# A transformer layer's feed-forward part in blocks of two by two with seven products instead of eight, on one Trainium2 core

## The chip, the core and the metric

The kernel runs on one core of one Trainium2 chip. The time is device microseconds (us) of one execution. The core has five engines with a queue of instructions each: TensorE (PE; its weight loads stand apart as PEld), VectorE (DVE), ScalarE (ACT), GpSimd (POOL) and SyncE (SP). They work side by side and wait for each other through semaphores. Transfers between the chip's main memory (DRAM) and the core's on-chip memory (SBUF) are issued from an engine's queue and carried by 16 DMA engines. TensorE writes its sums into eight accumulators ("banks", each 128 x 512 fp32), which the other engines read.

## The reference

One layer of an encoder, 512 tokens of 2048 features, everything in fp32. The second half of it, which the change is about, is cut out here:

```
proj = rmsnorm(x) @ w_in                  # 2048 x 8704: q, k, v of two attentions, two gates
A = windowed attention, B = neighbourhood attention on the token grid
x = x + (sigmoid(gA) * (A @ w_branch_a) + sigmoid(gB) * (B @ w_branch_b)) @ w_out
h2 = rmsnorm(x)
u = h2 @ w_up                             # 2048 x 11264
u = u[s-1] * cw[0] + u[s] * cw[1] + u[s+1] * cw[2] + conv_b      # along the tokens
gate, val = split(u, 2)                   # 5632 columns each
x = x + (silu(gate) * val) @ w_down       # 5632 x 2048
```

## The kernel before, in words

Activations are held transposed: a tile has 128 features on the partitions and the 512 tokens along the row. Every operand of a product is split into two float32r tiles, `hi` (rounded) and `lo` (the rest), and a product is three matmuls, hi·hi, hi·lo and lo·hi. So a 128 x 128 tile of weights times 512 tokens is three matmuls of 128 x 512, which one line issues (L74).

Weights stream in units of 512 KB. `stage` (L118) takes the next unit off a list that all the steps together make: it issues its load on SP's queue (L71; three `raw` buffers), then ACT's cast to `hi` (L135) and DVE's subtraction to `lo` (L136, 128 x 1024 each, two buffers each). `run_step` (L146) calls `stage` once per unit, ahead of the 24 matmuls of the unit that it uses itself, so that weights are always prepared one unit early, and at the end of a step it hands each of the four banks to the step's `evac`. A step makes 512 output columns. A list of queued closures (`run_queued`) runs attention's small work between units.

The order of the program: w_in's attention columns with the attentions (to about 600 us), gates of A, branch A, gates of B, branch B, output projection with the residual, and then the feed-forward part from about 1194 us on: `up` (L583) makes a chunk of 512 gate and 512 value columns, `conv` (L573) their evacuation, and `down` (L606) the product of one chunk earlier with the matching rows of w_down, added to the residual `x2` in SBUF (L610). In `conv`, DVE multiplies the bank by the norm's row factor (L575), ACT makes the middle tap with the bias (L576), and DVE adds the two outer taps (L577, L579). The sigmoid (L589) and the products of gate and value (L590, L595) follow, and `split` (L180, L181) makes the tiles for `down`.

The instruction order on each engine comes from a scheduler that simulates the program; loads through `dma` keep the program's order.

## Time and profile before

| what | value |
|---|---|
| median of 3 runs | 2634.89 us (2634.71 to 2635.88) |
| span of the profiled execution | 2634.1 us, 28831 instructions |
| TensorE busy | 2623.6 us (100%), granted clock 1.000 |
| weight loads | 2182.7 us (83%) |
| VectorE busy | 1258.4 us (48%) |
| ScalarE busy | 840.8 us (32%) |
| DMA, mean | 102 GB/s |

The profiled execution's own time is its span, from the first to the last instruction; it lies 0.8 us under the median of the runs. Times that are worked out from the trace go by the span. In a group's row, the columns behind the bar are the busy time of all its instructions, the mean time of one in ns, and how long the engine stood idle just before them and for what. The busy time of TensorE counts overlapping matmuls' ends, so the distance from one matmul to the next is read from a stretch of them, and not from the mean time of one.

### The profile page before, as it was taken

The page shows a single profiled execution, that of the slowest core. Times are in us where ns is not written, and L with a number is a line of the kernel's source. Part 1 is how long each engine was busy: PE and PEld are TensorE (multiplying, and loading weights), DVE is VectorE, ACT ScalarE, POOL GpSimd, SP SyncE. Part 2 cuts the span into 40 slices and gives each one's busy share as a digit, 9 for nine tenths or more (in the row PEclk, how much of TensorE's full clock was granted, in tenths as well). Part 3 has the DMA queues.
Part 4 walks back from the last instruction along what each step waited for, and adds up shares of the span by engine and source line. Part 5 has one row for each costly group of instructions (what it writes and reads, how often), then busy time and mean ns, then how long its engine had stood idle before and what let it go on. Part 6 is the DMA issues. An engine that isn't in the chain of part 4 may idle for free.

```text
span 2634.1 us, 28831 instructions
## 1 busy us (share of the span) xinstructions
PE 2623.6 (100%) x11848; PEld 2182.7 (83%) x11848; DVE 1258.4 (48%) x1685; ACT 840.8 (32%) x1156; POOL 34.4 (1%) x38
## 2 busy tenths in 40 slices
PE   9999999999999999999999999999999999999999
PEld 7888888888888888888888888888888888888887
DVE  6565545542333344435453636363636363636364
ACT  5355544532222222323232323231323232323231
POOL 0100000000000000000000000000000000000000
PEclk9999999999999999999999999999999999999999
DMA  5322222333233323332323232333333333332333
GB/s 181 96 89 85 90 94 90 114 107 115 98 96 96 112 96 127 113 114 94 96 96 101 95 100 97 96 96 96 96 97 98 100 97 96 96 97 96 96 96 128
DMA packets 152115, 268.53 MB, mean 102 GB/s; under 512 B 9520, under 2 KB 35120, under 8 KB 151984
## 3 DMA queue, kind: packets, MB, share of 16 engines
q1 hardware_dynamic: 147376, 258.31, 30.7%
q10 hardware_dynamic: 4608, 8.39, 0.8%
q8 instruction: 92, 1.51, 0.2%
q14 instruction: 39, 0.32, 0.0%
HBM read 258.27 MB, written 8.39 MB: 101 GB/s over the span
## 4 chain that ended last, share of the span: by engine, by line
PE 100%; DMA 0%; DVE 0%; ACT 0%; issue 0%; SPq 0%; ACTq 0%
PE mm L74 96%; PE tr L74 2%; PE tr L430 1%; PE tr L288 0%; PE tr L337 0%; DMA s<-in_x_t 0%; PE mm L217 0%; PE tr L217 0%; PE mm L208 0%; ACT s L183 0%; DVE s L514 0%; DVE s L610 0%; PE tr L208 0%; ACT hi L135 0%; SPq L71 0%
## 5 line engine op out<-in xcount | busy, mean ns | idle before, releaser
L74 PE MATMUL mm<-s,hi 128*128 128x512 f32 x6528 | 1937.0, 389 | 0.9 <-DVE s L514 0.9
L74 PEld LDWEIGHTS mm<-s,hi 128*128 128x128 f32 x6528 | 1224.5, 188 | 253.7 <-ACT s L524 1.3
L74 PE MATMUL mm<-s,lo 128*128 128x512 f32 x3264 | 1193.7, 389 | 0.0
L136 DVE TENSOR_TENSOR lo<-raw,hi 128x1024 fp32r<-128x1024 f32 (+1 forms) x465 | 568.1, 1222 | 1161.7 <-ACT hi L135 1159.1
L135 ACT CAST hi<-raw 128x1024 fp32r<-128x1024 f32 (+1 forms) x465 | 489.1, 1052 | 1507.3 <-PE mm L74 1332.7
L74 PEld LDWEIGHTS mm<-s,lo 128*128 128x128 f32 x3264 | 612.6, 188 | 126.6
L74 PE MATMUL mm<-hi,s 128*128 128x512 f32 x896 | 285.5, 395 | 5.8 <-ACT hi L135 5.8
L74 PEld LDWEIGHTS mm<-hi,s 128*128 128x128 f32 x896 | 168.6, 189 | 39.0 <-ACT hi L135 5.8
L74 PE MATMUL mm<-lo,s 128*128 128x512 f32 x448 | 176.8, 396 | 0.0
L610 DVE TENSOR_TENSOR e<-mm,e 128x512 f32<-128x512 f32 x132 | 90.1, 689 | 23.5 <-PE mm L74 23.2
L74 PEld LDWEIGHTS mm<-lo,s 128*128 128x128 f32 x448 | 84.9, 190 | 16.5
L576 ACT ACTIVATE s<-t,smalls 128x512 f32<-128x512 f32 x88 | 71.4, 811 | 42.6 <-DVE t L575 42.6
L577 DVE SCALAR_TENSOR_TENSOR s<-t,smalls,s 128x511 f32<-128x511 f32 x88 | 65.8, 748 | 10.1 <-ACT s L576 9.7
L579 DVE SCALAR_TENSOR_TENSOR s<-t,smalls,s 128x511 f32<-128x511 f32 x88 | 65.9, 749 | 2.4
L575 DVE TENSOR_TENSOR t<-mm,row 128x512 f32<-128x512 f32 x88 | 60.4, 687 | 2.4 <-PE mm L74 2.4
L435 DVE TENSOR_TENSOR pl<-tr,ph 128x256 fp32r<-128x256 f32 (+1 forms) x64 | 30.2, 485 | 29.7 <-ACT ph L434 29.6
L589 ACT ACTIVATE t<-s 128x512 f32<-128x512 f32 x44 | 27.8, 631 | 51.0 <-DVE s L579 51.0
L409 ACT ACTIVATE p<-p,nm 128x256 f32<-128x256 f32 (+1 forms) x64 | 35.4, 555 | 23.8 <-DVE nm L402 15.9
L434 ACT CAST ph<-tr 128x256 fp32r<-128x256 f32 (+1 forms) x64 | 26.1, 421 | 47.4 <-PE tr L74 22.1
L610 DVE TENSOR_TENSOR s<-mm,s 128x512 f32<-128x512 f32 x44 | 30.4, 692 | 19.9 <-PE mm L74 19.9
L74 PE MATMUL tr<-ph,s 128*128 128x256 f32 (+1 forms) x128 | 37.7, 313 | 0.0
L180 ACT CAST s<-s 128x512 fp32r<-128x512 f32 x52 | 32.0, 619 | 17.5 <-DVE s L531 9.7
(102 smaller groups left out, 849.8 us busy)
## 6 DMA issues: line engine op xcount, KB each, us to landing
raw<-in_w_up SPq DMA_DIRECT2D x176, 512.0 KB, 3.5
raw<-in_w_in SPq DMA_DIRECT2D x103, 512.0 KB, 3.6
raw<-in_w_down SPq DMA_DIRECT2D x88, 512.0 KB, 3.6
raw<-in_w_in SPq DMA_DIRECT2D x66, 256.0 KB, 3.1
raw<-in_w_out SPq DMA_DIRECT2D x32, 512.0 KB, 3.7
raw<-in_w_branch_a SPq DMA_DIRECT2D x16, 512.0 KB, 3.6
raw<-in_w_branch_b SPq DMA_DIRECT2D x16, 512.0 KB, 3.7
s<-in_x_t SPq DMA_DIRECT2D x20, 256.0 KB, 6.1
```

What stands on the lines that cost most here:

```text
L74: nc.tensor.matmul(o, l, r, start=start, stop=stop, skip_group_check=True)
L135: nc.scalar.copy(hi[:, c:c + n], raw[:, c:c + n])
L136: nc.vector.tensor_tensor(lo[:, c:c + n], raw[:, c:c + n], hi[:, c:c + n].bitcast(F32), ALU.subtract)
L180: nc.scalar.copy(hi, src)
L409: nc.scalar.activation(pr[j][:, :n], pr[j][:, :n], AF.Exp, bias=nm[:, j:j + 1], accum_out=sm[:, j:j + 1])
L435: nc.vector.tensor_tensor(pl[:, :n], b[:, :n], ph[:, :n].bitcast(F32), ALU.subtract)
L575: nc.vector.tensor_tensor(u, ps, rows["f"], ALU.mult)
L576: nc.scalar.activation(o, u, AF.Identity, bias=cb[:, idx:idx + 1], scale=cw[:, idx, 1:2])
L577: nc.vector.scalar_tensor_tensor(o[:, 1:], u[:, :S - 1], cw[:, idx, 0:1], o[:, 1:], op0=ALU.mult, op1=ALU.add)
L579: nc.vector.scalar_tensor_tensor(o[:, :S - 1], u[:, 1:], cw[:, idx, 2:3], o[:, :S - 1], op0=ALU.mult, op1=ALU.add)
L589: nc.scalar.activation(sg, g, AF.Sigmoid)
L610: nc.vector.tensor_tensor(x2[m], ps, x2[m], ALU.add)
```

## The change

The feed-forward products are made in blocks of two by two: two tiles of features by two halves of the weight columns on the one side, two tiles of features by two halves of 256 tokens on the other. For w_up the two column halves are the gate and the value columns; for w_down they are the two halves of its 2048. Instead of eight block products there are seven, each of a sum of weight blocks with a sum of activation blocks (Strassen's scheme in Winograd's form), and the four output blocks are sums of the seven.

- **Weights.** `Twin` loads two units at once: four planes of 128 x 512, 256 KB each. `add` makes three further planes on DVE out of them (L568 on 1024 elements, L570 and L571 on 512), which makes seven. `Product.prep` casts one unit's seven planes to `wh` on ACT (L612, 1024 and 768 elements) and subtracts to `wl` on DVE (L613, likewise).
- **Early sums.** For the first two up steps and for all of w_down (52 twins) the sums are made ahead, by `make_early` in the stretch between the attentions and the feed-forward part: load, `add`, and a store of four planes (1 MB) on GpSimd's queue (L581). They are read back when they are needed (1 MB of sums beside three raw planes).
- **Activations.** `forms` makes the seven blocks of a pair of tiles: 4 sums on DVE, 7 casts on ACT (L630) and 7 subtractions on DVE (L631), all 128 x 256. There are 30 pairs (8 for w_up, 22 for w_down).
- **Products.** A step has one bank for each of the seven products, and for each unit 7 x 2 x 3 = 42 matmuls of 128 x 256 (L77). There are 22 up steps of eight units, each giving two tiles of gate and two of value, and then 12 down steps (two parts of four steps with eight units, one of four with six): 11,088 matmuls of 128 x 256 in place of 6,336 of 128 x 512. Outside the feed-forward part the matmuls are the same.
- **Evacuation.** `combine` makes the four output blocks with one copy on ACT (L674) and seven sums on DVE (L675 to L681, 512 elements each). In `conv`, DVE multiplies by the row factor (L825, 1024 elements), and ACT makes all three taps (L829, L831, L832, two instructions each). The outer taps are added to the middle one by two DMAs on GpSimd's queue that accumulate in SBUF (L833, L834). Silu (L849), the product of gate and value (L850) and a store to DRAM (L851, GpSimd's queue) follow; `form_down` reads it back.
- **Down.** All up steps come first. The residual lies in DRAM (`total`); a down step's results are added to it by accumulating DMAs on GpSimd's queue, and in the last part by DVE ahead of the output.
- **Around it.** Branch A comes right after the first half of its gates, and its heads are read back and split just ahead of it (`before_a`); the other half of the gates is applied afterwards. There are 56 instead of 60 activation slots, and the raw stream's buffers give their place to the product weights' (`wst_ctx.close()`, in `post` of the last output step).

The diff, cut to its core:

```diff
+UP_EARLY = (0, 1)
...
+    def prep_to(n, **kw):
+        for u in units[at["prep"]:n + 1]:
+            if isinstance(u, Product) and "w" not in ffn:
+                return
+            u.prep(**kw)
+            at["prep"] += 1
+    def advance():
+        prep_to(at["use"] + 1)
+        while at["sums"] < len(twins) and twins[at["sums"]].first <= at["use"] + 2:
+            if "f" not in ffn:
+                return
+            twins[at["sums"]].sums()
+            at["sums"] += 1
+        while at["load"] < len(twins) and twins[at["load"]].first <= at["use"] + 4:
+            if at["early"] < len(early):
+                break
+            twins[at["load"]].load()
+            at["load"] += 1
+        make_early()
...
+    class Twin:
+        def __init__(self, w, d, c, first, kept):
+            self.w, self.first = w[d][:, :, :, :, c:c + 256], first
+            self.kept = kept and dram.tile([P, 4, 512], F32, name=f"sums{first}")
+        def fetch(self, *planes):
+            self.f = ffn["f"].tile([P, 7, 512], F32, tag="f", name="f", bufs=2)
+            for f, a, h in ((0, 0, 0), (1, 1, 0), (3, 0, 1), (6, 1, 1)):
+                if f in planes:
+                    dma(self.f[:, f].rearrange("p (b n) -> p b n", b=2), self.w[:, :, a, h])
+        def load(self):
+            if self.kept:
+                self.fetch(0, 1, 6)
+                dma(self.f[:, 2:6], self.kept)
+            else:
+                self.fetch(0, 1, 3, 6)
+        def add(self):
+            f = self.f
+            nc.vector.tensor_tensor(
+                f[:, 2:4], f[:, 0:7:6], f[:, 3].unsqueeze(1).to_broadcast([P, 2, 512]), ALU.add)
+            nc.vector.tensor_tensor(f[:, 4], f[:, 2], f[:, 6], ALU.add)
+            nc.vector.tensor_tensor(f[:, 5], f[:, 4], f[:, 1], ALU.add)
...
+        def keep(self):
+            nc.gpsimd.dma_start(self.kept, self.f[:, 2:6])
+    def make_early():
+        if "f" not in ffn or at["early"] == len(early) and not made:
+            return
+        if made and made[0][1] == 1:
+            made.popleft()[0].keep()
+        elif made and made[0][1] == 0 and (len(made) == 2 or at["early"] == len(early)):
+            made[0][0].add()
+            made[0][1] = 1
+            return
+        while len(made) < 2 and at["early"] < len(early):
+            t = early[at["early"]]
+            t.fetch_all()
+            made.append([t, 0])
+            at["early"] += 1
+    class Product:
+        def __init__(self, twin, i):
+            self.twin, self.s = twin, slice(i * 256, i * 256 + 256)
+        def prep(self):
+            self.parts = []
+            for tag, a, b in (("a", 0, 4), ("b", 4, 7)):
+                hi = ffn["w"].tile([P, b - a, 256], F32R, tag="h" + tag, name="wh", bufs=2)
+                lo = ffn["w"].tile([P, b - a, 256], F32R, tag="l" + tag, name="wl", bufs=2)
+                f = self.twin.f[:, a:b, self.s]
+                nc.scalar.copy(hi, f)
+                nc.vector.tensor_tensor(lo, f, hi.bitcast(F32), ALU.subtract)
+                self.parts += [(hi[:, i], lo[:, i]) for i in range(b - a)]
+    def forms(src):
+        y = src.rearrange("p j (t n) -> p (j t) n", t=2)
+        t = quad("o").rearrange("p j (t n) -> p (j t) n", t=2)
+        nc.vector.tensor_tensor(t[:, 0], y[:, 3], y[:, 1], ALU.subtract)
+        nc.vector.tensor_tensor(t[:, 1], y[:, 0], y[:, 1], ALU.subtract)
+        nc.vector.tensor_tensor(t[:, 2], t[:, 0], y[:, 0], ALU.add)
+        nc.vector.tensor_tensor(t[:, 3], t[:, 2], y[:, 2], ALU.subtract)
+        res = []
+        for v in (y[:, 0], y[:, 2], t[:, 0], t[:, 1], t[:, 2], y[:, 3], t[:, 3]):
+            o = slot(F32R)
+            nc.scalar.copy(o[:, :256], v)
+            nc.vector.tensor_tensor(o[:, 256:], v, o[:, :256].bitcast(F32), ALU.subtract)
+            res.append(o)
+        return res
+    def products(w, c, pairs, acts, evac, before=None, kept=False):
+        def run():
+            ps = []
+            for i, j in enumerate(pairs):
+                if before:
+                    before(i)
+                u = next_unit()
+                for f, (wh, wl) in enumerate(u.parts):
+                    if i == 0:
+                        ps.append(bank("mm"))
+                    a = acts[j][f]
+                    for m in range(2):
+                        o, s = ps[f][:, m * 256:(m + 1) * 256], slice(m * P, (m + 1) * P)
+                        mm(o, wh[:, s], a[:, :256], i == m == 0, False)
+                        mm(o, wh[:, s], a[:, 256:], False, False)
+                        mm(o, wl[:, s], a[:, :256], False, i == len(pairs) - 1 and m == 1)
+                if i == len(pairs) - 1:
+                    combine(ps, evac)
+                advance()
+                run_queued(1)
+            if before:
+                before(len(pairs))
+        steps.append(run)
+        v = w.rearrange("(d b a p) (h n) -> d p b a h n", b=2, a=2, p=P, h=2)
+        for j in pairs[::2]:
+            t = Twin(v, j // 2, c, len(units), kept)
+            twins.append(t)
+            units.extend(Product(t, i) for i in range(2))
+            if kept:
+                early.append(t)
+    def combine(ps, evac):
+        q1, q2, q7, q5, q6, q3, q4 = [p.rearrange("p (m n) -> p m n", m=2) for p in ps]
+        v = lambda: scratch().rearrange("p (m n) -> p m n", m=2)
+        top, low, p1, u3 = quad("u"), quad("u"), v(), v()
+        left, right = slice(0, 256), slice(256, 512)
+        nc.scalar.copy(p1, q1)
+        nc.vector.tensor_tensor(top[:, :, left], q2, p1, ALU.add)
+        nc.vector.tensor_tensor(p1, p1, q6, ALU.subtract)
+        nc.vector.scalar_tensor_tensor(u3, q7, -1.0, p1, op0=ALU.mult, op1=ALU.subtract)
+        nc.vector.tensor_tensor(low[:, :, right], u3, q5, ALU.subtract)
+        nc.vector.tensor_tensor(p1, p1, q5, ALU.add)
+        nc.vector.tensor_tensor(top[:, :, right], q3, p1, ALU.add)
+        nc.vector.tensor_tensor(low[:, :, left], u3, q4, ALU.subtract)
+        evac(top, low)
...
+    def before_a():
+        end_attention()
+        split_out(oa, out_a)
...
+        def post():
+            if n == 3:
+                wst_ctx.close()
+                ffn["w"] = ctx.enter_context(
+                    tc.tile_pool(name="w", bufs=2, side="right", reuse_waits="tile"))
+                prep_to(at["use"] + 1)
+                form_pair(6)
+                form_pair(7)
...
+    pairs_ff = D_FF // 256
+    act = [dram.tile([P, 2, S], F32, name=f"act{j}") for j in range(pairs_ff)]
+    def conv(u, idx):
+        o, before, after = quad("o"), quad("a"), quad("a")
+        nc.vector.tensor_tensor(
+            u, u, rows["f"].unsqueeze(1).to_broadcast([P, 2, S]), ALU.mult)
+        for m in range(2):
+            i = idx + m
+            nc.scalar.activation(
+                o[:, m], u[:, m], AF.Identity, bias=cb[:, i:i + 1], scale=cw[:, i, 1:2])
+            nc.scalar.activation(before[:, m], u[:, m], AF.Copy, scale=cw[:, i, 0:1])
+            nc.scalar.activation(after[:, m], u[:, m], AF.Copy, scale=cw[:, i, 2:3])
+        nc.gpsimd.dma_start(o[:, :, 1:], before[:, :, :S - 1], accum_op=ALU.add)
+        nc.gpsimd.dma_start(o[:, :, :S - 1], after[:, :, 1:], accum_op=ALU.add)
         return o
+            def out_part():
+                g, v = held["g"], held["v"]
+                nc.scalar.activation(g, g, AF.Silu)
+                nc.vector.tensor_tensor(v, g, v, ALU.mult)
+                nc.gpsimd.dma_start(act[s], v)
+            queue.extend((gate_part, lambda: None, lambda: None, val_part,
+                          lambda: None, lambda: None, out_part))
+        def before(i):
+            if s == 0 and i == 5:
                 rows["f"] = row_factor("f")[1]
+            if s == pairs_ff - 1 and i >= 1:
+                form_down(0, i - 1)
+        products(w_up, s * 256, range(8), h2, evac, before=before, kept=s in UP_EARLY)
...
+    def down(part, pairs, nxt=()):
+        last = not nxt
+        skip = len(pairs) - len(nxt)
+        for s in range(4):
+            old = []
+            def evac(top, low, s=s, old=old):
+                for h, t in enumerate((top, low)):
+                    if not last:
+                        nc.gpsimd.dma_start(total[h][s], t, accum_op=ALU.add)
+                    else:
+                        nc.vector.tensor_tensor(t, t, old[h], ALU.add)
+                        m = 8 * h + 2 * s
+                        nc.scalar.dma_start(
+                            out[m * P:(m + 2) * P].rearrange("(m p) n -> p m n", p=P), t)
+            def before(i, s=s, old=old):
+                if last and i == len(pairs) - 2:
+                    for h in range(2):
+                        old.append(quad("a"))
+                        dma(old[h], total[h][s])
+                if s == 3:
+                    for n in FORM[part][i]:
+                        form_down(part + 1, n)
+            products(w_down, s * 256, pairs, down_forms[part], evac, before=before, kept=True)
+    down_forms = {0: {}, 1: {}, 2: {}}
+    def form_down(part, j):
+        a = quad("a")
+        dma(a, act[j])
+        down_forms[part][j] = forms(a)
+    FORM = {0: [()] + [(8 + i,) for i in range(8)],
+            1: [()] + [(16 + i,) for i in range(6)] + [(), ()],
+            2: [()] * 9}
+    for s in range(pairs_ff):
+        up(s)
+    down(0, range(0, 8), range(8, 16))
+    down(1, range(8, 16), range(16, 22))
+    down(2, range(16, 22))
```

**VectorE at the end of a step.** Before, where four gate or value banks are evacuated (t: scratch, s: activation slot, row: the row factor):

```order
L575 TENSOR_TENSOR t_9610<-mm_9335,row_9204 128x512
L595 TENSOR_TENSOR s_9576<-s_9296,s_9576 128x512
L136 TENSOR_TENSOR lo_9548<-raw_9546,hi_9547 128x1024
L181 TENSOR_TENSOR s_9584<-s_9576,s_9583 128x512
L577 SCALAR_TENSOR_TENSOR s_9587<-t_9588,smalls_94,s_9587 128x511
```

With the change, where the seven banks of an up step are combined (f: a twin's planes, wh and wl: prepared weights, u: the combined blocks):

```order
L676 TENSOR_TENSOR t_12623<-t_12623,mm_12211 128x512
L613 TENSOR_TENSOR wl_12634<-f_12413,wh_12633 128x1024
L570 TENSOR_TENSOR f_12521<-f_12521 128x512
L613 TENSOR_TENSOR wl_12638<-f_12413,wh_12637 128x768
L677 SCALAR_TENSOR_TENSOR t_12624<-mm_12197,t_12623 128x512
L571 TENSOR_TENSOR f_12521<-f_12521 128x512
L678 TENSOR_TENSOR u_12622<-t_12624,mm_12204 128x2x256
L679 TENSOR_TENSOR t_12623<-t_12623,mm_12204 128x512
L681 TENSOR_TENSOR u_12622<-t_12624,mm_12225 128x2x256
L613 TENSOR_TENSOR wl_12711<-f_12521,wh_12710 128x1024
L680 TENSOR_TENSOR u_12621<-mm_12218,t_12623 128x2x256
```

Weight preparation and weight sums stand between the seven sums that free the banks.

**TensorE at the start of a step.** Before, a new step's matmuls begin in four other banks than the ones just finished (mm_9032 is the last bank of the step before):

```order
L74 MATMUL mm_9032<-s_9022,hi_9207 128x512
L74 MATMUL mm_9032<-s_9023,hi_9207 128x512
L74 MATMUL mm_9032<-s_9022,lo_9208 128x512
L74 MATMUL mm_9332<-s_8147,hi_9237 128x512
L74 MATMUL mm_9332<-s_8148,hi_9237 128x512
```

With the change, twelve rows behind the last matmul of the step before:

```order
L77 MATMUL mm_12675<-s_8760,wh_12571 128x256 x2
L77 MATMUL mm_12675<-s_8760,wl_12572 128x256
L77 MATMUL mm_12661<-s_8888,wh_12633 128x256 x2
L77 MATMUL mm_12668<-s_8891,wh_12633 128x256 x2
L77 MATMUL mm_12675<-s_8894,wh_12633 128x256 x2
L77 MATMUL mm_12682<-s_8763,wh_12571 128x256 x2
```

Seven of eight banks are in use in a step. The first three products of the step's first unit and then parts of its second unit (wh_12633) stand ahead of the first unit's fourth product (mm_12682).

**ScalarE and GpSimd behind a step.** Before, a middle tap stood between two casts (L135) at a time. With the change, ScalarE has, behind the three taps of the first of two gate tiles:

```order
L829 ACTIVATE o_13127<-u_13099,smalls_98 128x512
L831 ACTIVATE a_13128<-u_13099,smalls_98 128x512
L832 ACTIVATE a_13129<-u_13099,smalls_98 128x512
L829 ACTIVATE o_13304<-u_13100,smalls_98 128x512 x2
L612 CAST wh_13358<-f_13122 128x1024
L612 CAST wh_13300<-f_13122 128x768
L612 CAST wh_13362<-f_13122 128x768
L831 ACTIVATE a_13305<-u_13100,smalls_98 128x512 x2
```

and GpSimd's queue, for one up step:

```order
L833 DMA o_10737<-a_10738 128x2x511
L834 DMA o_10737<-a_10739 128x2x511
L833 DMA o_10914<-a_10915 128x2x511
L834 DMA o_10914<-a_10916 128x2x511
L851 DMA act1_134<-o_10914 128x1024
```

Eight tap instructions now stand between two casts (the three ahead of these rows and the first five here), and the store of a step's product (L851) stands behind its four adding transfers.

257 lines of the change are left out of this document (143 added, 114 removed).

## The prediction

> **What bounds the kernel now.** First the page's busy shares with the granted clock, and the chain of work that ended last with its last long step, whose columns are start, length, engine and work:
>
> ```profile
> span 2634.1 us, 28831 instructions
> PE 2623.6 (100%) x11848; PEld 2182.7 (83%) x11848; DVE 1258.4 (48%) x1685; ACT 840.8 (32%) x1156; POOL 34.4 (1%) x38
> PEclk9999999999999999999999999999999999999999
> PE 100%; DMA 0%; DVE 0%; ACT 0%; issue 0%; SPq 0%; ACTq 0%
> ...
> 1227.18 1403.09 PE mm L74 x6190
> ```
>
> TensorE is never kept waiting, and its clock is full throughout. 1403.09 us for 6190 matmuls is 0.2267 us for each of 512 columns. Next, busy times by stretch (columns: stretch, length, then busy time and count of PE, PEld, DVE, ACT, POOL; clock, DMA share, GB/s): the one ahead of the feed-forward part, and that part:
>
> ```profile
> 600.00:1190.00 590.00, 590.00 (x2604) 488.55 (x2603) 218.30 (x242) 155.91 (x182) 0.00 (x0) 1.00 0.33 106
> 1193.80:2630.00 1436.20, 1436.20 (x6346) 1189.34 (x6344) 702.84 (x844) 395.38 (x442) 1.93 (x1) 1.00 0.31 98
> ```
>
> The feed-forward part is 1436.2 us, 55% of the span, with DVE at 49%. So only less TensorE work shortens it, and DVE has as much room again.
>
> **The change, part by part.**
>
> *TensorE.* 6336 matmuls of 512 columns become 11,088 of 256. These exist before only in the attention; rows of several in a stretch, where one row's time is (n - 1) distances and one whole matmul, then the matmul alone (the mean in its group), and the shortest kind of load and matmul:
>
> ```profile
> 131.68 0.75 PE L74 MATMUL tr<-s 128*128 128x256 f32 x5
> 254.92 0.53 PE L74 MATMUL tr<-s 128*128 128x256 f32 x3
> L74 PE MATMUL tr<-s 128*128 128x256 f32 x96 | 17.0, 281 | 0.0
> 1219.27 0.95 PE L208 MATMUL mm<-ones,sq 128*128 128x1 f32 x8
> ```
>
> (0.75 - 0.281) / 4 = 0.117 us, (0.53 - 0.281) / 2 = 0.125, and for eight loads with one column each about (0.95 - 0.239) / 7 = 0.10. Half of 0.2267 is 0.113. I take 0.118, near the longer stretch: 11,088 x 0.118 = 1308 us, 128 under 1436. An up step (8 x 42 matmuls) is then at least 39.65 us.
>
> *DVE and ACT in an up step.* What the pieces cost, by their nearest rows:
>
> ```profile
> L136 DVE TENSOR_TENSOR lo<-raw,hi 128x1024 fp32r<-128x1024 f32 x463 | 566.8, 1224 | 1161.7 <-ACT hi L135 1159.1 <-PE mm L74 2.2
> L595 DVE TENSOR_TENSOR s<-s 128x512 f32<-128x512 f32 x44 | 30.2, 687 | 0.8
> L610 DVE TENSOR_TENSOR e<-mm,e 128x512 f32<-128x512 f32 x132 | 90.1, 689 | 23.5 <-PE mm L74 23.2
> L281 DVE TENSOR_TENSOR qr<-t 128x256 f32<-128x256 f32 x8 | 3.4, 420 | 0.0
> L135 ACT CAST hi<-raw 128x1024 fp32r<-128x1024 f32 x463 | 487.8, 1054 | 1507.3 <-PE mm L74 1332.7 <-issue 170.9 <-DMA raw<-in_w_in 1.1
> L326 ACT COPY s<-mm 128x512 f32<-128x512 f32 x8 | 4.7, 583 | 4.1 <-PE mm L74 4.1
> L576 ACT ACTIVATE s<-t,smalls 128x512 f32<-128x512 f32 x88 | 71.4, 811 | 42.6 <-DVE t L575 42.6
> L577 DVE SCALAR_TENSOR_TENSOR s<-t,smalls,s 128x511 f32<-128x511 f32 x88 | 65.8, 748 | 10.1 <-ACT s L576 9.7
> L183 ACT ACTIVATE s<-e,smalls 128x512 fp32r<-128x512 f32 x12 | 8.6, 715 | 5.8 <-DVE e L563 5.8
> ```
>
> 768 elements on DVE: halfway, (1.224 + 0.687) / 2 = 0.955. Per step, DVE has eight preparations, 8 x (1.224 + 0.955) = 17.4; four twins' sums, 4 x (1.224 + 2 x 0.687) = 10.4; seven sums of `combine`, 7 x 0.69 = 4.8; two row factors and the product of gate and value, 3 x 1.224 = 3.7. Sum 36.3 us, 92% of TensorE's 39.65. ACT: 8 x (1.054 + 0.82) = 15.0 for casts (768 again halfway, with 0.583 at 512), 0.6 for the copy, 4 x 0.811 + 8 x 0.715 = 9.0 for twelve taps, 1.05 for Silu: 25.7, 65%.
>
> The outer taps leave DVE (eight of L577's form, 8 x 0.748 = 6.0, which would have put it over TensorE), the weight sums come on. What margin is left can be used up by waiting. In the program's order a step's first matmuls need three banks that `combine` frees, its fourth product waits for L677, the fifth for L679, the seventh for L680. Walked with the times above, L677 ends 2.9 us into the step against 2.8 when TensorE gets there, L679 5.9 against 5.7, L680 8.5 against 9.2: about even, since preparation stands between these sums on DVE's queue, and a late sum holds TensorE with everything behind it. Two things then idle DVE itself. ACT's four middle and four outer taps, 4 x 0.811 + 4 x 0.715 = 6.1 us, stand ahead of a cast that DVE's next subtraction waits for; it has 3.5 us of other work in that time, so 2.6 are lost. And the planes of a twin have two buffers: a new megabyte can only be asked for when the last subtraction of the twin two earlier is done. Landing times:
>
> ```profile
> raw<-in_w_up SPq DMA_DIRECT2D x176, 512.0 KB, 3.5
> raw<-in_w_in SPq DMA_DIRECT2D x66, 256.0 KB, 3.1
> s<-in_x_t SPq DMA_DIRECT2D x20, 256.0 KB, 6.1
> q1 hardware_dynamic: 147376, 258.31, 30.7%
> out_a<-o ACTq DMA_DIRECT2D x8, 256.0 KB, 2.0
> ```
>
> Four planes of 256 KB take between 3.5 (a 512 KB transfer) and 6.1 us (loads that queue up in fours); I take 4.5, against 2.9 us of work that DVE has meanwhile: 1.6 lost. With 1 us of handing over between ACT and DVE, DVE's loop is 36.3 + 2.6 + 1.6 + 1 = 41.5 us, and a step 42, at worst 44. Bounds: 39.65 if order and buffers absorb all of it. Steps 0 and 1 have their sums ready: 40.5.
>
> *Down.* A pair's forms are 4 sums and 7 subtractions of 256 elements at 0.420. Counted in the order of DVE's instructions from one step's `combine` to the next one's, with these prices, DVE has 40.7 us in the last up step (14 of the forms' subtractions of part 0), 55.8 in the first down step (42 of them), 40.1 to 40.3 in three later ones (25 to 31 each), and 18 to 25 in the other eight, where it sets nothing. I take 43 for that up step, 57, 3 x 42, 4 x 40.6 (TensorE's 39.65 and a wait for a bank) and 4 x 30.5 for steps of six units (252 x 0.118 = 29.7): 57 + 126 + 162 + 122 = 467. Up is 2 x 40.5 + 19 x 42 + 43 = 922. Together 1389 us, 47 under 1436 and 81 over the floor. Bounds: the floor below; 2 us more in each of 30 steps, 1450, above.
>
> *Ahead of it.* Branch A's heads are read back and split right ahead of its matmuls, which nothing covers: +3 us. The weights' pool takes the raw stream's place only after the last output matmul; the first cast and subtraction (2.3 us) and a late twin: +6. The early sums: 52 x (1.224 + 2 x 0.687) = 135 us of DVE in a stretch of 590 where it is busy 218, so hidden; its traffic rises from 106 GB/s by 2 MB for every second unit (10.9 us), 192 GB/s, to about 300, where the queue's 258 MB in 30.7% of the span make 320 GB/s at full use. Raw loads then queue behind a twin's on SP, but are asked for a unit early: 0 taken, up to 30 us if it fails.
>
> *The end.* Before, the last matmul is followed by
>
> ```profile
> 2630.30 0.69 DVE L610 TENSOR_TENSOR s<-mm,s 128x512 f32<-128x512 f32 x1 [0.67 <-PE mm L74]
> 2627.85 3.51 ACTq L612 DMA_DIRECT2D out_x<-s  x4
> ```
>
> With the change by the copy, the chain of `combine`, two additions of 1024 elements (0.6 + 4 x 0.69 + 2 x 1.2 = 5.8) and a 512 KB store, 3.5 to 4: 10 us, before about 4.
>
> Sum: 1194 + 3 + 6 + 1389 + 10 = **2602 us** of span, 32 under 2634.1; the runs' median stands 0.8 above the span, so 2603.
>
> The Trainium skill, "TensorE: Matmul & The Clock Gate", section "Wait — 56ns, not 53.3ns?", says that with hardware decoding off TensorE's sequencer spends about 62 ns on each matmul; if a weight load costs the same, a pair would take 124 ns, an estimate from that page, and 11,088 of them 1375 us, 67 more than my floor. The row at 131.68 us shows 0.117 per pair, which speaks against it, but five pairs may have been queued ahead.
>
> **Rivals.**
>
> 1. *The order absorbs everything:* TensorE never waits. For it: before, DVE held it hardly ever. Against: 92% is not 49%. 1194 + 3 + 1308 + 10 = 2515, with 0.115 per matmul 2482.
>
> 2. *The adding DMAs are late (slower than before).* In `conv` the outer taps are two transfers of 128 x 2 x 511 elements on GpSimd's queue, one behind the other, and the second waits for the first; Silu, the gate product and the release of the `o`, `a` and `u` buffers wait for them, and the next step's `combine` needs `u`. The value pair's are issued some 27.8 us into the step, and the gate product (L850) stands on DVE's queue at 34.4, with the next unit's subtraction behind it: they have 6.5 us for two. No row shows an accumulating transfer or one on this queue. Plainly, 512 packets of 88 ns over 16 engines (147,376 packets in 30.7% of 16 x 2634 us) are 2.8 us, a 512 KB load lands in 3.5, the loads in fours in 6.1. Each us beyond 6.5 is a us of TensorE in 22 steps: at 8 us, +33, the gain is gone; at 10 us, 2603 + 77 = 2680. For it: reading the destination as well doubles the traffic. Against: 6.5 us is over twice the plain price. The Trainium skill warns of this in "SBUF — State Buffer", section "SBUF: two separate sides": GpSimd's DMA descriptors are starved while DVE holds the port that they share. No run shows it here.
>
> 3. *The shorter matmul is dearer:* the row at 254.92 us with its 0.125. For it: it is as much a row as the other, and a five-in-a-row stretch may draw on matmuls that were queued ahead. Against: the two rows' ends are rounded to 0.01 us, which over two distances is 0.005 each. 1194 + 3 + 11,088 x 0.125 + 10 = 2593 without waits, and with half of the forecast's 81 us of waits (a slower TensorE needs the banks later) and the 6 us at the start about 2640, no gain.
>
> 4. *The early sums choke the raw stream,* or something not listed: 2603 + 30, up to 2690.
>
> **How the numbers follow.** Forecast 0.42 (own range 2575 to 2630); order absorbs everything 0.22; adding DMAs or the DVE chain late 0.22; dearer matmul 0.08; early sums and the rest 0.06. The range of 8 in 10 runs from 2535, since a partly absorbed step of 40.5 is 2570 and the floor 2515 holds a part of the second case, to 2690 for the third. This kernel's measurement can tell 0.2%, 5.3 us, from no change. Faster: the forecast nearly whole, the second, and little of the others: 0.62; within 0.2% 0.06; slower 0.32.
>
> **What would show it.** TensorE's share falls under 100%, and the 128 x 256 groups show their idle time as released by DVE, L677 and L679 above all; the distance between steps' first matmuls is about 42 us, with DVE busy near 90% of it. A step of 39.7 shows the first rival. A landing time of the `o<-a` transfers above 6.5 us, with L850 idle for DMA, shows the second; a distance of 0.125 within a unit, without idle time, the third. Gaps of TensorE for `raw` between 600 and 1190 us show the fourth. I am wrong if DVE is under 85% and TensorE waits all the same.

## The result: slower by 6%

The changed kernel takes 2793.06 us (2786.35 to 2800.03, 4 runs) against 2635.38 us before: a ratio of 1.0599, 95% interval 1.0581 to 1.0617. The forecast was 2603 us, with 2690 as its upper end.

The head of its page answers to the first three rows that the prediction began with:

```profile
span 2789.6 us, 41803 instructions
PE 2604.5 (93%) x16600; PEld 2358.9 (85%) x16600; DVE 1748.1 (63%) x2399; ACT 1206.8 (43%) x1783; POOL 202.6 (7%) x232
PEclk9999999999999999999999999999999988999999
```

TensorE's busy time fell by only 19 us, and it now stands idle for 185. The first row below is the stretch ahead of the feed-forward part (compare 600 to 1190 us before); then come the up steps, the first down step, and the other down steps:

```profile
600.00:1200.00 600.00, 569.94 (x2399) 455.56 (x2399) 326.52 (x396) 151.93 (x189) 31.72 (x59) 0.99 0.81 282
1262.64:2284.70 1022.06, 925.56 (x7368) 908.50 (x7369) 725.49 (x848) 519.04 (x673) 111.04 (x103) 0.96 0.58 148
2284.70:2361.30 76.60, 48.14 (x353) 47.52 (x352) 48.61 (x95) 41.12 (x79) 7.69 (x7) 0.80 0.73 213
2361.30:2780.40 419.10, 407.93 (x3387) 404.31 (x3385) 275.14 (x400) 183.13 (x268) 14.27 (x17) 1.00 0.73 228
```

| part, us | before | forecast | changed kernel |
|---|---|---|---|
| up to the first feed-forward matmul | 1193.8 | 1203 | 1262.6 |
| up steps | | 922 | 1022 |
| down steps | | 467 | 496 |
| feed-forward part | 1436 | 1389 | 1518 |
| behind the last matmul | 4 | 10 | 9 |

So both parts lost: 69 us ahead of the feed-forward part, 82 in it. An up step, from one `combine` to the next, is 46.86 us on the mean of 20, where TensorE's own work is 336 x 0.119 = 40.0 (0.119 us is the distance of two matmuls that wait for nothing).

Who keeps whom waiting in the up steps (columns: us in all, times, longest), TensorE, then VectorE, then ScalarE:

```profile
PE mm L77 <- DVE wl L613: 43.0, 29, 5.4
PE mm L77 <- ACT wh L612: 38.9, 21, 7.6
PE mm L77 <- DVE t L676: 13.0, 11, 4.5
...
DVE wl L613 <- ACT wh L612: 125.3, 33, 11.1
DVE f L568 <- DMA f<-in_w_up: 103.1, 45, 6.0
DVE o L850 <- DMA o<-a: 39.5, 15, 5.1
...
ACT a L832 <- DMA o<-a: 74.3, 20, 7.5
...
ACT a L831 <- DMA o<-a: 44.1, 16, 4.7
```

TensorE waits far more for prepared weights (the first two rows, 81.9 us) than for free banks (the third, 13.0). The three rows are 94.9 us, 4.5 in each of 21 steps; of the rest of the 6.9 us above 40.0, the lower clock can explain up to 0.04 x 46.9 = 1.9, since 0.96 was granted over these steps. VectorE waits for ScalarE's casts, and ScalarE, ahead of them on its queue, for the adding DMAs (`o<-a`), whose `a` buffers it fills again. Beside that VectorE waits at the weight sums (L568) for planes that are on their way, and at the gate product (L850) for the adding DMAs. Rows of one step, each engine's in order of time: GpSimd's queue, then those of ScalarE and VectorE that bear on it, then TensorE's one long wait:

```profile
1838.25 1.17 POOL L833 DMA_DIRECT2D o<-a  x1 [19.61 <-ACT a L831]
1845.63 1.18 POOL L834 DMA_DIRECT2D o<-a  x1 [6.20 <-ACT wh L612]
1846.81 1.22 POOL L833 DMA_DIRECT2D o<-a  x1
1856.46 1.18 POOL L834 DMA_DIRECT2D o<-a  x1 [8.42 <-DMA o<-a]
...
1851.10 1.34 ACT L832 ACTIVATE a<-u,smalls 128x512 f32<-128x512 f32 x2 [2.88 <-DMA o<-a]
...
1842.68 1.23 DVE L568 TENSOR_TENSOR f<-f 128x1024 f32<-128x1024 f32 x1 [4.05 <-DMA f<-in_w_up]
...
1854.14 1.83 DVE L613 TENSOR_TENSOR wl<-f,wh 128x768 fp32r<-128x768 f32 x2 [3.89 <-ACT wh L612]
1857.70 1.22 DVE L568 TENSOR_TENSOR f<-f 128x1024 f32<-128x1024 f32 x1 [1.73 <-DMA f<-in_w_up]
1863.90 1.23 DVE L850 TENSOR_TENSOR o<-o 128x1024 f32<-128x1024 f32 x1 [4.97 <-DMA o<-a]
...
1865.65 1.22 DVE L613 TENSOR_TENSOR wl<-f,wh 128x1024 fp32r<-128x1024 f32 x1
...
1866.92 0.58 PE L77 MATMUL mm<-s,wl 128*128 128x256 f32 x1 [5.37 <-DVE wl L613]
```

Four adding transfers fill nearly all the time from 1838.3 to 1863.9 us, 25.6 us of a step of 46.9; the third is issued 1.2 us behind the second, the second and the fourth only when the one ahead has landed. ScalarE's L832 of the value half waits for the gate's second one, casts stand behind it, and L613 at 1854.14 is late by that. L850 waits for the last one, and the L613 behind L850 is what ends TensorE's wait of 5.4 us.

### The profile page after: what moved, and what is told of

Its sections match the earlier page's. It is cut to its first block, busy times and chain, and to the rows that moved or that the text cites. A ratio compares the mean times of both kernels' runs of the same rounds, so it can differ in the third digit from the quotient of the medians.

```text
span 2789.6 us, 41803 instructions
## 1 busy us (share of the span) xinstructions
PE 2604.5 (93%) x16600; PEld 2358.9 (85%) x16600; DVE 1748.1 (63%) x2399; ACT 1206.8 (43%) x1783; POOL 202.6 (7%) x232
## 5 line engine op out<-in xcount | busy, mean ns | idle before, releaser
L77 PE MATMUL mm<-s,wh 128*128 128x256 f32 x7392 | 1316.4, 287 | 87.1 <-ACT wh L612 72.4
L77 PEld LDWEIGHTS mm<-s,wh 128*128 128x128 f32 x7392 | 1123.6, 193 | 97.8 <-ACT wh L612 78.6
L77 PE MATMUL mm<-s,wl 128*128 128x256 f32 x3696 | 963.6, 287 | 51.5 <-DVE wl L613 50.9
L612 ACT CAST wh<-f 128x1024 fp32r<-128x1024 f32 (+1 forms) x528 | 480.7, 938 | 566.8 <-PE mm L77 391.2
L613 DVE TENSOR_TENSOR wl<-f,wh 128x1024 fp32r<-128x1024 f32 (+1 forms) x528 | 564.6, 1089 | 256.9 <-ACT wh L612 249.9
L77 PEld LDWEIGHTS mm<-s,wl 128*128 128x128 f32 x3696 | 669.7, 192 | 62.5 <-DVE wl L613 61.2
L77 PE MATMUL mm<-s,hi 128*128 128x512 f32 x2304 | 700.7, 397 | 5.2 <-ACT hi L151 3.0
L77 PEld LDWEIGHTS mm<-s,hi 128*128 128x128 f32 x2304 | 436.1, 190 | 105.7 <-ACT hi L151 4.0
L77 PE MATMUL mm<-s,lo 128*128 128x512 f32 x1152 | 430.5, 400 | 26.9 <-DVE lo L152 26.9
L152 DVE TENSOR_TENSOR lo<-raw,hi 128x1024 fp32r<-128x1024 f32 (+1 forms) x201 | 244.2, 1218 | 239.9 <-ACT hi L151 239.1
L568 DVE TENSOR_TENSOR f<-f 128x1024 f32<-128x1024 f32 x132 | 161.6, 1224 | 273.7 <-DMA f<-in_w_down 166.0
L77 PE MATMUL mm<-hi,s 128*128 128x512 f32 x896 | 289.5, 399 | 5.6 <-ACT hi L151 5.6
L77 PEld LDWEIGHTS mm<-s,lo 128*128 128x128 f32 x1152 | 219.4, 190 | 83.9 <-DVE lo L152 34.2
L77 PEld LDWEIGHTS mm<-hi,s 128*128 128x128 f32 x896 | 168.6, 190 | 41.8 <-ACT hi L151 5.6
L77 PE MATMUL mm<-lo,s 128*128 128x512 f32 x448 | 178.7, 400 | 0.0
L77 PEld LDWEIGHTS mm<-lo,s 128*128 128x128 f32 x448 | 85.1, 190 | 18.4
L832 ACT ACTIVATE a<-u,smalls 128x512 f32<-128x512 f32 x88 | 60.5, 712 | 74.3 <-DMA o<-a 74.3
L570 DVE TENSOR_TENSOR f<-f 128x512 f32<-128x512 f32 x132 | 90.9, 689 | 1.5
L571 DVE TENSOR_TENSOR f<-f 128x512 f32<-128x512 f32 x132 | 90.9, 689 | 1.4
L833 POOL DMA_DIRECT2D o<-a x44 | 53.4, 1214 | 511.6 <-ACT a L831 410.0
L831 ACT ACTIVATE a<-u,smalls 128x512 f32<-128x512 f32 x88 | 60.5, 713 | 44.6 <-DMA o<-a 44.1
```

Of the source, the lines that this page charges most:

```text
L77: nc.tensor.matmul(o, l, r, start=start, stop=stop, skip_group_check=True)
L152: nc.vector.tensor_tensor(lo[:, c:c + n], self.raw[:, c:c + n], hi[:, c:c + n].bitcast(F32), ALU.subtract)
L568: nc.vector.tensor_tensor(f[:, 2:4], f[:, 0:7:6], f[:, 3].unsqueeze(1).to_broadcast([P, 2, 512]), ALU.add)
L570: nc.vector.tensor_tensor(f[:, 4], f[:, 2], f[:, 6], ALU.add)
L571: nc.vector.tensor_tensor(f[:, 5], f[:, 4], f[:, 1], ALU.add)
L612: nc.scalar.copy(hi, f)
```

## The experiments

A run without a ratio beside it is a single one. The four runs of the changed kernel lie up to 14 us apart, so a span that differs by less than that shows nothing by itself; the starts and steps within a trace are what the readings go by.

**The up steps: adding DMAs or the planes' reload.** First each of the two is left out. Without the adding DMAs:

```
-        nc.gpsimd.dma_start(o[:, :, 1:], before[:, :, :S - 1], accum_op=ALU.add)
-        nc.gpsimd.dma_start(o[:, :, :S - 1], after[:, :, 1:], accum_op=ALU.add)
```

> Left out: the two adding DMAs of each conv (L833, L834), so that the outer taps are computed on ScalarE but never added. With them an up step takes 46.8 us (2284.7 - 1301.4 over 21 steps). Theory A (four adding transfers, one behind the other from 1838.3 to 1863.9 us in the step looked at, hold ScalarE's L831/L832 and VectorE's L850, and through them the casts): a step falls to 41 to 42.5 us, the span by 90 to 125 us. Theory B (the reload of the weight planes, for which L568 waits 5.8 us in that step, sets the pace): the step stays above 45 us, the span falls by less than 40.

Measured: 43.42 us a step, a span of 2701.1 us (-88.5; the first down step is shorter too, 62 us against 77). Neither theory's figure: half of the excess is gone. Without the loads:

```
-                self.fetch(0, 1, 3, 6)
+                if len(held_f) < 2:
+                    self.fetch(0, 1, 3, 6)
+                    held_f.append(self.f)
+                else:
+                    held_f.append(held_f.pop(0))
+                    self.f = held_f[-1]
```

> Left out: the loads of w_up for the up steps from the third on; two tiles of planes are loaded once and used again and again (the sums are still made each time). Theory A: the step stays at 45 us or more, since the adding transfers stay. Theory B: 41 to 42.5 us. If both waits lie side by side and each alone is enough, both this run and the one without adding DMAs stay near 45.

Measured: 42.96 us a step, span 2705.8. Again a little over half of it. Both edits together:

> The changed kernel without the adding DMAs and without the loads of w_up from the third up step on. If the two waits in the up steps lie one behind the other, their gains add: from 46.8 us a step minus 3.0 (without the adding DMAs alone) and minus 4.4 (without the loads alone) is 39.4, which is under TensorE's 336 x 0.119 = 40.0, so 40 to 40.5. If they hide each other or share a third cause (the order of VectorE's work, its 36.3 us), the step stays at 42 or more.

Measured: 40.32 us a step, span 2637.3. Between 1320 and 2040 us TensorE has no gap left:

```profile
1320.00:2040.00 720.00, 720.00 (x6003) 720.00 (x6002) 603.16 (x679) 425.79 (x533) 9.64 (x18) 1.00 0.06 20
```

So the two waits, with the clock that they cost, are nearly the whole excess of the up steps: 3.4 and 3.9 us alone, 6.5 together. The transfers also slow each other, as the landing times show (columns: count, KB each, median us from issue to landing; the changed kernel, then without the loads, then without the adding DMAs, all from 1320 to 2200 us):

```profile
f<-in_w_up SPq DMA_DIRECT2D x300, 256.0 KB, 4.4
o<-a POOLq DMA_DIRECT2D x75, 511.0 KB, 6.7
```
```profile
o<-a POOLq DMA_DIRECT2D x82, 511.0 KB, 4.8
act<-o POOLq DMA_DIRECT2D x20, 512.0 KB, 2.9
```
```profile
f<-in_w_up SPq DMA_DIRECT2D x323, 256.0 KB, 4.0
```

An adding transfer lands in 4.8 us without the loads beside it and in 6.7 with them; a plain store of nearly the same size on the same queue takes 2.9 in both runs. The Trainium skill, "DMA: Bandwidth & Descriptors", section "Anatomy of one DMA — SWDGE (gpsimd) path", fits 2.0 us and the bytes at 436 GB/s for that queue, 3.2 us for 512 KB as an estimate from it: near the plain store, while the adding transfer takes half as much again. It also differs from the store in staying within SBUF, so how much of that is the adding isn't shown.

Was the reload a matter of the order on VectorE's queue? The sums are held behind the last subtraction issued so far:

```
-            if not self.kept:
-                self.add()
+            if not self.kept:
+                with tc.issue_after(last["prep"]) if "prep" in last else ExitStack():
+                    self.add()
```

> The changed kernel; one thing is added: a twin's three sums must stand on VectorE's queue behind the last weight subtraction (L613) issued so far, so that L568 no longer stands ahead of subtractions that could run while its planes are on their way. The load is asked for as before. Theory B1 (the reload costs time because L568 stands too early in the order): L568's idle time for the loads falls from 103 us over the up steps to under 30, and a step from 46.8 to 42.5 to 44 us, as without the loads (42.4). Rival (the load itself is too late, whatever the order): the step stays at 46 to 47, with the idle time moved to other rows.

Measured: L568's idle time for loads falls to 0.3 us, as said, but the step only to 46.16; ScalarE's L832 (L833 in that kernel) now waits 141 us for the adding DMAs (74 in the changed kernel):

```profile
ACT a L833 <- DMA o<-a: 141.3, 20, 8.5
```

The rival was right in that the idle time moves to other rows: with the wait at L568 gone, the one for the adding DMAs takes its place.

**The place of the weights.** In the changed kernel even the 128x512 matmuls that the change doesn't touch are slower: 0.2325 us from start to start (0.2269 before), from the first stretch on, without any wait. What differs there is where the weight buffers lie. In the kernel before, only that was changed:

```
-    wst = pool("wst", 3)
+    pool("edge", 1, side="right").tile([P, 8], F32, tag="edge", name="edge")
+    wst = pool("wst", 3, side="right")
```

> The kernel before with one thing changed: the weight stream's buffers (raw, hi, lo) lie at the other end of the memory, where the changed kernel has them. Theory E (where the weights lie makes every 128x512 matmul 0.2325 us instead of 0.2269): 10,920 x 0.0056 = 61, a span of about 2695 us. Rival F (something else in the changed kernel, as its transfers on GpSimd's queue): 2634 us and 0.2269.

Measured: a span of 2693.8 us. The long step of the chain that was 1403.09 us for 6190 matmuls before is now

```profile
1251.48 1438.45 PE mm L75 x6190
```

0.2324 us each: the place alone makes the unchanged kernel 2.3% slower. Region or offset? The same with a wider edge (`[P, 40]`), so that the weights' tiles begin 128 bytes lower; and the old place with 128 unused bytes between weights and activations:

> The kernel before with the weight buffers at the other end of the memory, but 128 bytes lower than in the last such run: the weights' tiles then begin at the same offset modulo 2048 as the activations' (1856), as in the kernel before; in the run that took 2693.8 us they began 128 bytes beyond it (1984). Theory G (the offset between the two matmul operands decides): 0.2269 us per matmul of 512, span 2634. Theory H (the region of the memory decides): 0.2324, span 2694.

> The kernel before with 128 unused bytes between the weight buffers and the activations, so that the weights stay at 1856 modulo 2048 in their old region and the activations begin at 1984. Theory G: about 0.232, span near 2694. Theory H: 0.2269, span 2634.

Measured: 2634.1 and 2693.5 us, with these rows, in this order:

```profile
1227.12 1403.09 PE mm L75 x6190
```
```profile
1251.19 1438.45 PE mm L75 x6190
```

In these four kernels the region doesn't matter, the offset between the two operands' tiles does. The changed kernel with the wider edge:

> The changed kernel with the weight buffers 128 bytes lower, nothing else. Theory G: its 512-column matmuls fall from 0.2325 to 0.2269 (4800 of them, 27 us), those of 256 columns by about half of that (0.1189 to 0.116 to 0.1175: 11,088, 15 to 30 us, less where TensorE waits anyway): a span of 2735 to 2765 us. Theory H: unchanged, 2785 to 2798.

Measured: 2782.9 us, less than expected. The 512-column matmuls are back at 0.2275, but the feed-forward part begins only 11 us earlier, at 1251.2: with the early sums still there, TensorE waits 35.4 us for the raw stream there instead of 29.9, and its clock is 0.98 instead of 0.99. Its 256-column matmuls go from 0.1189 to 0.1199 (means over those without a gap), and an up step stays at 46.85. That the place is the cause for these isn't shown: without loads and adding DMAs, at the changed kernel's own places, an up step without gaps took 40.32 / 336 = 0.1200 for each, too.

**The early sums.** All sums where they are used:

```
-UP_EARLY = (0, 1)
+UP_EARLY = ()
-            products(w_down, s * 256, pairs, down_forms[part], evac, before=before, kept=True)
+            products(w_down, s * 256, pairs, down_forms[part], evac, before=before, kept=False)
```

> No sums are made ahead of the feed-forward part: every twin, of w_down too, makes its own as the middle up steps do. Theory C (the early loads, sums and stores slow the raw stream): the feed-forward part begins near 1225 us instead of 1262.6, TensorE has no wait for L152 in the stretch from 600 us on, and its granted clock there is 1.00; the first two up steps are some 6 us longer each, and the down steps with forms grow by up to 10 us. Rival D (the early work is covered and the 69 us come from a slower matmul alone): the start moves by less than 15 us. Under D the 128x512 matmuls at 0.2325 us (0.2269 before) cost 4800 x 0.0056 = 27 us of the 69.

Measured: the feed-forward part begins at 1221.7 us, 41 earlier, and TensorE waits for nothing on the way there; the 28 that are left to 1193.8 are about the place's 27. (With the place mended and the early sums kept, the start was 1251.2, so the two don't simply add.) The first two up steps aren't longer, though 6 us more each were expected. The span is only 11 us shorter, 2778.6, since the down steps take 28 us more. What of the early work is in the way? In the changed kernel, from 600 us on, waits and then the group of the sums:

```profile
PE mm L77 <- DVE lo L152: 26.9, 15, 4.9
...
SPq L74 <- DMA sums<-f: 57.8, 17, 8.5
```
```profile
L568 DVE TENSOR_TENSOR f<-f 128x1024 f32<-128x1024 f32 x52 | 63.7, 1224 | 170.4 <-DMA f<-in_w_down 166.0 <-DMA f<-in_w_up 4.2
```

Two queues that the raw stream needs hold waits of the early work: SyncE's (loads of planes wait for a store, raw loads behind them) and VectorE's (L568 waits for planes, L152 behind it). First the loads of planes for the early sums (`fetch_all`) are issued on GpSimd's queue:

```
-            self.fetch(0, 1, 3, 6)
+            self.fetch(0, 1, 3, 6, queue=nc.gpsimd.dma_start)
```

> The changed kernel; only the loads of planes for the early sums are issued on GpSimd's queue, where the stores of the sums already are, instead of SyncE's. The bytes are the same. Theory J (head of the queue: raw loads stand behind plane loads that wait for a store's end): TensorE's waits for L152 and L151 between 600 and 1262 us, 30 us, fall under 8, and the feed-forward part begins between 1222 and 1232 us. Theory K (traffic: 282 GB/s in that stretch, raw loads landing in 5.9 to 6.6 us instead of 3.6): the waits stay above 20 us and the start above 1250.

Measured: TensorE's waits in the stretch are 38 us and the start is 1267.3: it isn't SyncE's queue alone. L568 still waits 144 us for its planes. Then, with the loads on SyncE again, the sums behind the raw stream's last subtraction (`last["plain"]`, L152):

```
-            made[0][0].add()
+            with tc.issue_after(last["plain"]):
+                made[0][0].add()
```

> The changed kernel; the early sums must stand on VectorE's queue behind the raw stream's last subtraction (L152) issued so far, two subtractions later than now. The traffic and all transfers' queues stay. Theory L (L568 waits on VectorE for its planes with L152 behind it): L568's idle time in the stretch falls from 170 us to under 60, TensorE's waits for L152 from 27 us to under 8, and the feed-forward part begins between 1225 and 1240 us. Theory K (traffic alone, raw loads landing in 6 us instead of 3.6): the waits stay above 20 us and the start above 1250.

Measured: far off, the start at 1642.7 us, span 3175.6. L568 waits no longer, but the later sums make the stores later, and SyncE waits for them:

```profile
SPq L74 <- DMA sums<-f: 534.1, 33, 19.6
```

Both edits together:

> The changed kernel with the loads of planes on GpSimd's queue and the early sums behind the raw stream's last subtraction on VectorE's: neither queue that the raw stream uses holds a wait of the early work any longer, and the bytes are the same. Theory M (two queues that take each other's place): TensorE's waits between 600 us and the feed-forward part fall under 8 us (32.2 in the changed kernel) and that part begins between 1222 and 1235 us. Theory K (traffic): waits above 20, start above 1250.

Measured: the start at 1232.8 us, as theory M has it; TensorE's waits are 11 us, where under 8 was expected, at the same traffic (286 GB/s, 282 in the changed kernel). The largest of them:

```profile
PE mm L77 <- DVE lo L152: 7.3, 5, 3.0
```

So three quarters of the 41 us come from waits on two queues, and taking them off one alone leaves them on the other or puts them there; at most 11 us are left for the traffic (1232.8 - 1221.7). The 52 sums need not cost what they did.

**A version that is faster.** From these: sums in the order of `order_only`; the value half's outer taps on VectorE again, by the old two instructions; sums made early only for three down steps, the first one and the last of each of the first two parts (12 twins; the expectation speaks of four steps); the raw weights' place mended, the product weights' left:

> Four things together: the order of the sums as in the run beside it; the value half's outer taps on VectorE again (two instructions of 511 for each tile, 3 us more a step, 39.3 in all), so that only the gate's go by adding DMAs, with nothing behind them; sums made early only for the 12 twins of the four down steps that also make forms (52 before); the raw stream's weights at 1856 modulo 2048 (1024 from the activations), the product weights where they were. From the runs so far: pre-feed-forward part 1222 (without early work) - 27 (place) + 12 x 0.8 = 1205; up steps 40.5 to 42: 22 x 41.3 = 908; first down step 60 to 76, three with forms 46.5, others 39.5 and 30: 370 + 60 to 76 + 50 = about 485; 10 at the end: 2590 to 2630, against 2635 before. If VectorE at 39.3 of 40.3 us still holds TensorE with every wait, the step is 44 and the span 2665.

Measured: 2693.72 us, ratio 1.0223 (1.0206 to 1.0240): the expected time was missed. The start, 1200.8 us, is near the expected one, but the step is 44.48, which is what was expected if VectorE had no slack. The trace has another candidate, one instruction: the gate's Silu (L860 there) waits on ScalarE for the adding DMAs, with casts behind it:

```profile
ACT o L860 <- DMA o<-a: 183.7, 21, 10.4
```

So it is held back to the end of the step (and the last up step, which isn't in the mean, has no adding DMAs):

```
-                nc.scalar.activation(g, g, AF.Silu)
+                with tc.issue_after(last["cast"]):
+                    nc.scalar.activation(g, g, AF.Silu)
...
-                          lambda: None, lambda: None, out_part))
+                          lambda: None, lambda: None, lambda: None, out_part))
```

> As the mixed kernel that took 2693.7 us, with the gate's Silu held back to the end of the step behind the casts of its last units (in that run Silu stood 183.7 us on ScalarE for the adding DMAs, with casts queued behind it, and an up step took 44.6 us), and with both halves' outer taps on VectorE in the last up step. Theory A (the adding DMAs' landing time, met on a queue with work behind it, is what is left): a step falls to 40.3 to 42 us, the span by 21 x 2.6 to 4.3 = 55 to 90 us, to 2600 to 2640. Rival (VectorE at 39.3 of 40.3 us leaves no slack): step 44, no change.

Measured: 2592.06 us, ratio to before 0.9839 (0.9805 to 0.9873): 1.6% under the kernel before, and a little better than expected. VectorE's lack of slack was not the cause. The step is 39.93 us, at TensorE's own 40:

```profile
1320.00:2040.00 720.00, 720.00 (x6070) 720.00 (x6069) 666.41 (x761) 390.64 (x472) 53.38 (x55) 1.00 0.54 146
```

With all outer taps on VectorE:

> The same with all outer taps on VectorE and no adding DMA in any up step. VectorE then has 42.3 us of work a step, more than TensorE's 40.3: 42.5 to 43.5 us a step if nothing else holds it, 2640 to 2665 in all. Below 42 would mean that the prices are too high, above 44 that something other than the adding DMAs and the order of the sums is still in the way.

Measured: 40.19 us a step, 2587.49 us, where 42.5 to 43.5 was expected. VectorE's work is less than its prices say; over 17.9 steps (720 / 40.19):

```profile
1320.00:2040.00 720.00, 719.47 (x6041) 717.83 (x6040) 698.58 (x827) 339.05 (x396) 9.57 (x18) 1.00 0.38 119
```

698.58 / 17.9 = 39.0 us a step, not 42.3. The adding DMAs by themselves cost nothing visible: with half of them, and no casts queued behind their wait (the run before), the step is about the same.

## Why the prediction was wrong, step by step

The sum was 2602 us and the span is 2789.6. Of the 188 us between them, 60 lie ahead of the feed-forward part, 100 in the up steps and 29 in the down steps, and the end took 1 less. Two steps failed above all: the up step's 42 us, which had no term for waits on the adding DMAs, and the early sums' 0.

- **TensorE's floor** was right: 0.118 taken, 0.1189 measured where nothing holds it, 10 us over the sum. The dearer matmul (0.125) and the estimate of 0.124 from the Trainium skill ("TensorE: Matmul & The Clock Gate", "Wait — 56ns, not 53.3ns?") are both above what was measured.
- **VectorE's 36.3 us a step** were too many: 725.49 us over 21.8 steps (1022.06 / 46.86) are 33.3. The price was the duration of one instruction, but neighbours overlap; these three begin 1.13 and 1.14 us apart:

```profile
1831.06 1.23 DVE L825 TENSOR_TENSOR u<-u,row 128x1024 f32<-128x1024 f32 x1
1832.19 1.23 DVE L568 TENSOR_TENSOR f<-f 128x1024 f32<-128x1024 f32 x1
1833.33 1.23 DVE L825 TENSOR_TENSOR u<-u,row 128x1024 f32<-128x1024 f32 x1
```

 A step's 38 instructions at up to 0.09 us less each are 3.4, enough for the 3 us. The trace of before hardly showed it, since VectorE there mostly waited ahead of each (1161.7 us of idle time before L136).
- **The step of 42 us** failed, in the right places but the wrong mechanism. It made VectorE's work the pace, and VectorE was busy 71% of the up steps (725.49 of 1022.06) while TensorE waited: the prediction's own sign of being wrong. The waits on banks (L676, L677) are 14 us in all; the 2.6 us for ScalarE's taps and 1.6 for the reload were there in kind, but what holds ScalarE is less its own taps' time than L831 and L832 waiting for `a` buffers, 118.4 us in all, for which the forecast had no term. 46.86 us became 40.32 with the adding DMAs and the reload left out, under the 41.5 that I gave VectorE's loop.
- **The second rival** had the adding DMAs and the side right, at a chance of 0.22. It asked that both value transfers be through within 6.5 us of 27.8; the first was issued 28.0 us into the step looked at (1846.81 - 1818.79) and the second ended 17 us later. TensorE's wait there came by the rival's path, through L850 and the subtraction behind it. Its price didn't hold: by its rule 17 us cost 10.5 us a step, but leaving the transfers out gave back 3.4 us with the loads there and 2.6 without them. It took the pair at 8 to 10 us (two transfers that land in 4.8 us each are 9.6, and beside the loads it was more), and it priced L850, which waited 39.5 us in all for the transfers, but not the longer waits at L831 and L832. VectorE had more slack than counted and the two waits partly lie side by side; how much each of these took off the price wasn't tried apart. Nor was it tried whether GpSimd's descriptors are starved by VectorE.
- **The early sums** were taken at 0, with up to 30 us if they fail: they cost 41. The 135 us of VectorE's work were hidden but for 11 us at most; what wasn't are the waits that stand on two in-order queues ahead of the raw stream.
- **The unchanged part** was taken at its old time. The 128 bytes cost it 4800 x 0.0056 = 27 us, a term that the sum didn't have. Of the 9 us that were added for branch A's heads and the weights' pool hardly anything is seen: without early sums the start was 1221.7, and 27 less is 1194.7.
- **Down** was 467 and is 496: the first step 77 us instead of 57, the two steps with forms 49 instead of 42, the plain ones 39 to 40 as said. 77 became 62 without the adding DMAs and 59 without the loads as well, so they hold the first down step too; through which buffers wasn't tried apart.

## What to carry to other kernels

A transfer that takes 7 us costs nothing until an instruction that waits for it stands ahead of work on an in-order queue; before pricing a change, list for each queue, SyncE's too, what waits there and what is behind it, and check that moving the wait doesn't put it on another queue. Price back-to-back vector instructions by the distance of their starts, and count a kernel's own streams when a new transfer's landing time is estimated. When a change moves buffers, compare the untouched instructions' durations first: here 27 us were lost, and could be had back, without touching the work.

## What the runs showed of the hardware

- The start-to-start time of a 512-column matmul depended on where its two operands' tiles lie to each other: 0.2267 us in the long stretch of the kernel before and with the weights in the other region of SBUF at its offset; 0.2324 with a shift of 128 bytes of either operand, in either region. No other shift was tried on its own, and the cause is open.
- The clock that was granted to TensorE falls with its waits: 0.96 over the up steps, 0.80 over the 77 us of the first down step, 1.00 between 1320 and 2040 us in the run without loads and adding DMAs, where it didn't wait. One wait of 2.3 us came before such a fall: behind one that ended at 1717.43 us in the changed kernel, the granted clock was 0.50 from 1718.41 to 1721.82, and 14 matmuls that began from 1718.51 to 1721.50 were 0.213 us apart instead of 0.119.
